# The sample tokens' sparse attention, four tokens at a time in the four column quarters of TensorE's array

## The chip, the cores and the metric

The kernel runs on one core of a Trainium2 chip, as one program. The metric is its time on the device in microseconds (us); less is better. The engines are TensorE (PE in the profile; PEld is its weight load), VectorE (DVE), ScalarE (ACT), GpSimdE (POOL) and SyncE (SP), whose queue issues most of the DMA transfers.

## The reference

One inference step of a four-layer decoder for 512 prompt positions and 8 sample tokens (one new position each, with 512 past positions in a cache). Layers 0 and 3 mix tokens by native sparse attention (NSA), layer 1 by a gated MLP, layer 2 by a linear recurrence (HGRN2); each is followed by a SwiGLU feed-forward block. All is float32. In an NSA layer 16 query heads of 64 channels share 4 key/value heads, and three branches (compressed, selected pages, window) are added under gates. With 512 past positions the nine blocks of 64 are fewer than the sixteen that may be selected, so a sample token reads all its pages. What the change touches is this part, for the 8 sample tokens:

```python
def masked_attend(q, k, v, mask):
    s = jnp.einsum('bqgrd,bkgd->bqgrk', q, k).astype(jnp.float32) * ATTN_SCALE
    p = jnp.where(mask, jax.nn.softmax(jnp.where(mask, s, NEG_INF), axis=-1), 0.0)
    return jnp.einsum('bqgrk,bkgd->bqgrd', p.astype(v.dtype), v), p
...
    s = jnp.einsum('bqgrd,bqgnjd->bqgrnj', q, k_sel).astype(jnp.float32) * ATTN_SCALE
    p = jax.nn.softmax(jnp.where(sel_mask, s.reshape(B, Tq, G, R, -1), NEG_INF), axis=-1)
    o_slc = jnp.einsum('bqgrnj,bqgnjd->bqgrd', p.reshape(s.shape).astype(v_sel.dtype), v_sel)
...
    o_win, _ = masked_attend(q, kw, vw, win_mask[None, :, None, None, :])
    return (gates[:, :, 0, ..., None] * o_cmp + gates[:, :, 1, ..., None] * o_slc
            + gates[:, :, 2, ..., None] * o_win)
```

## The kernel before

Activations lie with features on the 128 partitions and the 520 columns (512 prompt, 8 sample) along them. Every projection multiplies blocks of weights of 128 columns by two halves of the columns (256 and 264), in three passes (`mm`, L248 to L250), on float32r parts whose sum is exact. Weights come by SP's queue (`Weights.dma`, L87) and are split by ScalarE (L100) and VectorE or, beside attention's output projection, by GpSimdE (L101).

An NSA layer (`nsa`) has W_in (21 units of 128 columns, `nsa_in`), attention, and W_out (8 units, `nsa_out`). Attention is written as generators whose steps are put between other instructions by hand; the order of the code's steps is the order of the program, on each engine. `compress` builds the compressed keys and values (L821). `attend` is the prompt's attention by groups, blocks of 128 queries and branches: scores on TensorE (L947, L915), masking and minimum on VectorE (L949), exp on ScalarE (L951), scaling on three engines (L960, L963), transposes (L982), a split by ScalarE and VectorE (L985, L986), and products with the values (L998). Part of it runs beside W_in. After W_in a loop gives one step of `attend` and one of `fill`, which takes steps of `sample` and `compress` in turn, until half the prompt is done; then W_out's first half of columns starts, with four of these steps at each tick (every six projection matmuls).

`sample` is the attention of the 8 sample tokens, on rows (token, head): row 16 b + h, so two tokens lie in each quarter of 32 rows. `begin(1)` and `begin(2)` make the scores and the softmax of the selected pages and of the window, `end(1)` and `end(2)` the products with the values; all add up in one PSUM bank `O`. Scores: for each token `b` and each half `v` of the key channels, one float32 matmul (L1078) of the token's 32 query columns (`Qp`, zero for the other token of the quarter) with its 512 keys, into the 32 PSUM rows of its quarter. Values: for each token and each 128 of its positions, one float32 matmul (`acc`, L1042) of 32 probability columns (`PT`) with 256 value channels. Each matmul uses 32 of the array's 128 columns, the quarter `r = b // 2 * 32`:

```python
for b, t in rows(br, 0):
    kb = t.rearrange("p n (v c) -> p n v c", v=2)
    r = b // 2 * 32
    for v in range(2):
        nc.tensor.matmul(S[r:r + 32], Qp[:, v, b], kb[:, :, v], start=b % 2 == 0 and v == 0,
                         stop=b % 2 == 1 and v == 1)
        yield
```

`rows` loads keys or values on SP's queue, five tokens ahead in the order: four pages of 128 KB for the selected branch (`page`, L763, `cache_slc`), one transfer of 512 KB for the window (L1067, `cache_win`). Tiles named `g` come from one pool of 38 buffers, so a load goes out when the earlier reader of its buffer is done. PSUM tiles (`ps`) come from eight banks.

Of the kernel before, what the change touches and what calls it, by code (L numbers as in the profile page):

```python
# [19 lines left out]
EPS = 1e-5  # L20
CH = (8, 7, 7)
NFF = sum(CH)
SLOTS = 38        # tiles of the pool that nearly everything lives in
WM, WV = 3, 0     # layer norm: ticks before the mean's and the variance's matrix products
# HGRN: order of a head's four projections (q, forget gate, v, output gate), units that run by halves first, ticks
# before a head's levels, levels built ahead, ticks of the sample's part, rate of the last head, output units beside it
HORD, HF, HW, BUILD, SW0, SWAIT, HRATE, EARLY = (0, 1, 2, 3), 6, 1, 3, 0, 8, 2, 6
# NSA: units between scores and mix, blocks between transposes and values, steps that exp and the like are put off
LAG, PVLAG, DEFER = 2, 3, 1
# NSA: steps a tick of attention (beside W_in, beside W_out) and of compression, and of the others for one of attention  # L30
RATE, RATE2, CRATE, STEPS = 4, 4, 1, 1
# NSA: steps that the sample's pages, values and compressed rows are waited for, tokens whose pages load ahead
CWAIT, EWAIT, AHEAD = 8, 5, 5
# [8 lines left out]
def alternate(*gs):  # L42
    """Steps of some generators in turn, until all end."""
    live = list(gs)
    while live:
        for x in list(live):
            try:
                next(x)
                yield
            except StopIteration:  # L50
                live.remove(x)


def wait(n):
    for _ in range(n):
        yield
# [12 lines left out]
class Weights:  # L69
    """Streams weight blocks: DMA, then a split in two float32r parts, ahead of their use."""  # L70
# [46 lines left out]
class Split:  # L117
    """Activations by blocks of features, as two float32r parts whose sum is exact."""
# [25 lines left out]
class Net:  # L144
# [67 lines left out]
    def spawn(self, g, rate=1.0):  # L212
        """A generator whose steps are issued between those of the matrix products."""
        self.par.append([g, rate, 0.0])
        return g
# [21 lines left out]
    def mm(self, unit, nk, R, half, ks=None, p=None):  # L237
        """One 128-column block of weights times the columns of a half: three passes a block of rows."""
        nc = self.nc
# [16 lines left out]
    def order(n, first, last):  # L256
        """(index, half): the first and the last few by halves, the others both halves together."""
# [5 lines left out]
    def ln(self, cols, li, sums, pair, X=None, out=None, direct=False):  # L263
        """Layer norm over the features, in place; its split goes to X, or out(j, c0, c1, pair) follows each pair.
        With direct, the tensor engine alone sums the squares."""
# [61 lines left out]
    def table(self, i):  # L327
        """The set of ScalarE's tables that the next functions need: one set for exp and ln together."""
# [6 lines left out]
    def guess(self, ys, vs):  # L335
        """y = exp(-ln(var + EPS) / 2), guesses at 1 / sqrt(var + EPS)."""
# [6 lines left out]
    def newton(self, ys, vs):  # L343
        """A Newton step from the guesses, and -2 times the results."""
# [19 lines left out]
    def out_proj(self, units, nk, R, scale, li, first=0, last=7, final=False, early=0):  # L364
        """x = scale * x + W h by blocks of features; with li the layer norm runs behind it."""
# [154 lines left out]
    def bounds(self):  # L520
        """The heads' lower bounds of the forget gates, and the norm's gain."""
# [24 lines left out]
    def hgrn(self, layer, plan):  # L546
# [26 lines left out]
        def sample(h, QK, FV, G, S0):  # L573
            """The sample tokens of a head: their states one step on, and what they read from them."""
# [28 lines left out]
        def head(h, QK, FV, G, smp):  # L603
# [6 lines left out]
            def build(i):  # L610
                """Queries times decays from a block's start, keys times decays to its end, by doubling blocks."""
# [23 lines left out]
            def odd(ap, i):  # L635
                """Columns in the second halves of the blocks of a level: its queries."""
# [128 lines left out]
    def nsa(self, layer, plan):  # L765
# [49 lines left out]
        def summaries(cm, n, b):  # L815
            """Compressed keys and values of n pages; with b == 8, of the prompt, whose last page is the position term."""
# [16 lines left out]
        def compress():  # L833
            """Of the prompt first, then of each token's pages."""
# [560 lines left out]
```

## Time and profile before

| | |
|---|---|
| time, median of 3 runs | 3125.0 us (3124.13 to 3129.43) |
| profiled execution: span from first to last instruction | 3127.9 us |
| profiled execution: own time | not given apart from its span |
| TensorE busy | 2960.0 us, 95% |
| VectorE busy | 1734.5 us, 55% |
| ScalarE busy | 1296.0 us, 41% |
| GpSimdE busy | 472.8 us, 15% |
| mean granted clock of TensorE | 0.979 of full speed |
| DMA | 280.61 MB, mean 90 GB/s |

A line of the timeline has the start, the time to the last end, the engine, the line of the code, the operation, what it writes and reads, the shape (weights' rows*columns, then rows x moving columns) and how many records it merges; in brackets stands the idle time ahead of it and what ended it. A float32 matmul gives two records. Ends of matmuls are modelled, so a busy TensorE need not be at its peak.

### The profile page before, as it was taken

What the parts mean: (1) busy time and instruction counts of PE and PEld (TensorE: products, weight loads), DVE (VectorE), ACT (ScalarE), POOL (GpSimd) and SP (SyncE); (2) the same over time, 40 slices, a digit from 0 to 9 for tenths busy, and PEclk for the clock granted to TensorE, in tenths of its full rate; (3) what the DMA queues carried; (4) which work ended last, traced back from release to release, by engine and by line L of the source; (5) the groups of instructions that cost most, each with busy time, mean ns of one, the idle gap of its engine ahead of it and who ended that gap; (6) DMA issues with size and microseconds to landing.
All of it is one profiled execution on the core that took longest, in us unless ns stands there. A gap on an engine that the chain in (4) does not pass through costs nothing. (4 is left out here: it accounts for less than half of the span.)

```text
span 3127.9 us, 56300 instructions
## 1 busy us (share of the span) xinstructions
PE 2960.0 (95%) x22730; PEld 2772.8 (89%) x22730; DVE 1734.5 (55%) x3821; ACT 1296.0 (41%) x2902; POOL 472.8 (15%) x446
## 2 busy tenths in 40 slices
PE   8898999999989999999899999999899999999997
PEld 8887468999988999998899889999888865799997
DVE  4887545333456633337777773333668866543334
ACT  4666434322345431234455443223456655332322
POOL 0222032000030300004222130000312212300002
PEclk9999999999999999999999999999999999999999
DMA  4222433223222222322222222232122143323221
GB/s 170 74 61 84 135 108 102 88 84 107 82 82 95 67 90 92 98 86 78 76 83 76 71 95 88 92 104 82 68 79 66 60 150 91 132 83 100 89 83 40
DMA packets 136039, 280.61 MB, mean 90 GB/s; under 512 B 13026, under 2 KB 76002, under 8 KB 135778
## 3 DMA queue, kind: packets, MB, share of 16 engines
q1 hardware_dynamic: 127168, 261.86, 26.6%
q10 hardware_dynamic: 7458, 10.95, 1.0%
q0 software_dynamic: 1152, 4.19, 0.5%
q8 instruction: 179, 2.93, 0.4%
q14 instruction: 82, 0.67, 0.1%
HBM read 263.69 MB, written 13.27 MB: 89 GB/s over the span
## 5 line engine op out<-in xcount | busy, mean ns | idle before, releaser
L248 PE MATMUL ps<-g 128*128 128x256 f32 (+1 forms) x6176 | 1784.2, 289 | 14.5 <-ACT g L100 13.2
L249 PE MATMUL ps<-g 128*128 128x256 f32 (+1 forms) x6176 | 1755.4, 284 | 6.8 <-DVE g L101 6.8
L250 PE MATMUL ps<-g 128*128 128x256 f32 (+1 forms) x6176 | 1757.1, 285 | 4.4 <-DVE g L271 2.7
L248 PEld LDWEIGHTS ps<-g 128*128 128x128 f32 x6176 | 1177.7, 191 | 37.9 <-ACT g L100 15.0
L249 PEld LDWEIGHTS ps<-g 128*128 128x128 f32 x6176 | 1177.3, 191 | 13.1 <-DVE g L101 8.3
L250 PEld LDWEIGHTS ps<-g 128*128 128x128 f32 x6176 | 1175.1, 190 | 6.1 <-DVE g L271 3.5
L101 DVE TENSOR_TENSOR g<-g 128x512 fp32r<-128x512 f32 (+1 forms) x708 | 468.6, 713 | 59.8 <-ACT g L100 52.5
L100 ACT CAST g<-g 128x512 fp32r<-128x512 f32 (+1 forms) x788 | 426.6, 608 | 118.9 <-DVE g L101 98.0
L419 DVE TENSOR_TENSOR row<-row,ps 128x256 f32<-128x256 f32 (+1 forms) x176 | 74.8, 425 | 515.7 <-PE ps L250 515.7
L209 ACT CAST g<-row 128x256 fp32r<-128x256 f32 (+1 forms) x192 | 78.6, 410 | 503.2 <-DVE row L419 491.6
L360 POOL TENSOR_TENSOR row<-x 128x256 f32<-128x256 f32 (+1 forms) x16 | 13.0, 812 | 1451.7 <-DVE x L383 1331.5
L418 ACT ACTIVATE row<-ps 128x256 f32<-128x256 f32 (+1 forms) x176 | 67.6, 384 | 334.3 <-PE ps L250 334.0
L951 ACT ACTIVATE g<-g,nst 128x128 f32<-128x128 f32 (+3 forms) x256 | 143.1, 559 | 109.8 <-DVE nst L949 109.3
L381 DVE SCALAR_TENSOR_TENSOR x<-x,ps 128x256 f32<-128x256 f32 (+1 forms) x128 | 52.9, 423 | 167.9 <-PE ps L250 167.8
L963 POOL TENSOR_SCALAR g<-g,nst 128x128 f32<-128x128 f32 (+3 forms) x64 | 76.5, 1195 | 442.7 <-DVE nst L956 378.7
L998 PE MATMUL ps<-g 128*128 128x512 f32 x384 | 141.4, 451 | 0.0
L949 DVE CUSTOM_DVE_ANT_0 g<-ps,ncst 128x128 f32<-128x128 f32 (+3 forms) x256 | 119.1, 482 | 39.4 <-PE ps L947 34.1
L947 PE MATMUL ps<-g 128*128 128x256 f32 (+2 forms) x512 | 123.9, 343 | 11.3 <-DVE nst L949 5.9
L985 ACT CAST g<-ps 128x512 fp32r<-128x512 f32 x160 | 91.9, 583 | 102.2 <-PE ps L982 83.2
L101 POOL TENSOR_TENSOR g<-g 128x512 fp32r<-128x512 f32 x80 | 105.0, 1333 | 172.8 <-ACT g L100 170.1
L383 DVE TENSOR_TENSOR x<-x,ps 128x256 f32<-128x256 f32 (+1 forms) x128 | 53.8, 424 | 135.5 <-PE ps L250 135.4
L210 DVE TENSOR_TENSOR g<-row,g 128x256 fp32r<-128x256 f32 (+1 forms) x192 | 81.7, 429 | 83.8 <-ACT g L209 83.8
(239 smaller groups left out, 2954.2 us busy)
## 6 DMA issues: line engine op xcount, KB each, us to landing
g<-ffn_in SPq DMA_DIRECT2D x176, 512.0 KB, 3.6
g<-ffn_out SPq DMA_DIRECT2D x64, 448.0 KB, 3.3
g<-nsa_in SPq DMA_DIRECT2D x42, 512.0 KB, 3.8
cm<-cache_cmp SPq DMA_DIRECT2D x64, 256.0 KB, 3.8
g<-cache_slc SPq DMA_DIRECT2D x128, 128.0 KB, 2.6
g<-cache_win SPq DMA_DIRECT2D x32, 512.0 KB, 6.5
g<-ffn_out SPq DMA_DIRECT2D x32, 512.0 KB, 3.5
g<-hgrn_in SPq DMA_DIRECT2D x32, 512.0 KB, 3.9
```

Of the source, the lines that this page charges most:

```text
L100: self.nc.scalar.copy(h[:, a:b], r[:, a:b])
L101: (self.sub[a > 0] or self.nc.vector).tensor_sub(l[:, a:b], r[:, a:b], h[:, a:b].bitcast(FT))
L209: self.nc.scalar.copy(h, src)
L210: self.nc.vector.tensor_sub(l, src, h.bitcast(FT))
L248: nc.tensor.matmul(p[:, :n], H[:, s], a, start=k == 0, stop=False)
L249: nc.tensor.matmul(p[:, :n], L[:, s], a, start=False, stop=False)
L250: nc.tensor.matmul(p[:, :n], H[:, s], b, start=False, stop=k == nk - 1)
L947: nc.tensor.matmul(p[:, :nn], q, kt[:, s, :nn], start=s == 0, stop=s == 1)
L949: nc.vector.tensor_tensor_reduce(P, p[:, :n], tri[:, 512 - n:], 1.0, 3e38, OP.add, OP.min, st[:, i:i + 1])
L951: defer(lambda P=P, i=i: (self.table(LN_EXP), nc.scalar.activation(P, P, AF.Exp, bias=st[:, i:i + 1], scale=-1.0, accum_out=st[:, 4 + i:5 ...
L985: nc.scalar.copy(PT[:, 0, :512], p)
L998: nc.tensor.matmul(o, v, PT[:, s, :512], start=start and s == 0, stop=stop and s == 1)
```

## The change

`rows` goes through the tokens in the order 0, 2, 4, 6, 1, 3, 5, 7 and gives them out four at a time, the first four when six tokens' loads are issued, the others after the first four's use. `begin` issues, for each four and each `v`, four matmuls next to each other, one in each column quarter; `end` does so for each four and each 128 positions. Ahead of each such group the generator passes two steps in which it issues nothing (`QWAIT`). The changed file also drops comments, and its lines are moved: L1078 is L1083 there, L1042 is L1043, L763 is L764, L1067 is L1068, L982 is L983, L998 is L999, L248 to L250 are L249 to L251.

```diff
-CWAIT, EWAIT, AHEAD = 8, 5, 5
+CWAIT, EWAIT, AHEAD, QWAIT = 8, 5, 5, 2
...
             def rows(br, v):
...
                 ts = []
-                for b in range(8 + AHEAD):
-                    if b < 8:
-                        t = self.flat()[:, :1024].rearrange("p (n c) -> p n c", n=4)
-                        if br == 1:
-                            for n in range(4):
-                                self.page(4 * b + n, t[:, n, :], a["cache_slc"][lj, v])
-                        else:
-                            nc.sync.dma_start(t, a["cache_win"][lj, v, b])
-                        ts.append(t)
-                    if b >= AHEAD:
-                        yield b - AHEAD, ts.pop(0)
+                for i, b in enumerate((0, 2, 4, 6, 1, 3, 5, 7)):
+                    t = self.flat()[:, :1024].rearrange("p (n c) -> p n c", n=4)
+                    if br == 1:
+                        for n in range(4):
+                            self.page(4 * b + n, t[:, n, :], a["cache_slc"][lj, v])
+                    else:
+                        nc.sync.dma_start(t, a["cache_win"][lj, v, b])
+                    ts.append((b, t))
+                    if i == AHEAD:
+                        yield ts[:4]
+                        del ts[:4]
+                yield ts
 
             def begin(br):
                 S = self.ps()
-                for b, t in rows(br, 0):
-                    kb = t.rearrange("p n (v c) -> p n v c", v=2)
-                    r = b // 2 * 32
+                for four in rows(br, 0):
                     for v in range(2):
-                        nc.tensor.matmul(S[r:r + 32], Qp[:, v, b], kb[:, :, v], start=b % 2 == 0 and v == 0,
-                                         stop=b % 2 == 1 and v == 1)
+                        yield from wait(QWAIT)
+                        for b, t in four:
+                            kb = t.rearrange("p n (v c) -> p n v c", v=2)
+                            r = b // 2 * 32
+                            nc.tensor.matmul(S[r:r + 32], Qp[:, v, b], kb[:, :, v], start=b % 2 == 0 and v == 0,
+                                             stop=b % 2 == 1 and v == 1)
                         yield
...
-                for b, vb in values:
-                    r = b // 2 * 32
+                for four in values:
                     for n in range(4):
-                        acc(O[r:r + 32, :256], PT[:, n, b], vb[:, n])
+                        yield from wait(QWAIT)
+                        for b, vb in four:
+                            r = b // 2 * 32
+                            acc(O[r:r + 32, :256], PT[:, n, b], vb[:, n])
                         yield
```

**TensorE, first scores of the selected pages in layer 0.** The scores are written to `ps_3829`; `g_3830` holds the keys of token 0, `g_3835` those of token 1 before and of token 2 in the change; L982 and L998 (L983 and L999) are attention's transposes and products. Before:

```order
L1078 MATMUL ps_3829<-g_3830,g_3824 32x512
L982 MATMUL ps_3861<-ident_85,g_3579 128x128 x2
L982 MATMUL ps_3861<-ident_85,g_3580 128x128 x2
L998 MATMUL ps_3576<-g_3629,g_3000 128x512 x2
L1078 MATMUL ps_3829<-g_3830,g_3824 32x512
L982 MATMUL ps_3880<-ident_85,g_3579 128x128 x2
L982 MATMUL ps_3880<-ident_85,g_3580 128x128 x2
L998 MATMUL ps_3576<-g_3644,g_3000 128x512 x2
L1078 MATMUL ps_3829<-g_3835,g_3824 32x512 x2
```

In the change:

```order
L1083 MATMUL ps_3829<-g_3830,g_3824 32x512
L1083 MATMUL ps_3829<-g_3835,g_3824 32x512
L1083 MATMUL ps_3829<-g_3840,g_3824 32x512
L1083 MATMUL ps_3829<-g_3845,g_3824 32x512
L983 MATMUL ps_3923<-ident_85,g_3579 128x128 x2
L983 MATMUL ps_3923<-ident_85,g_3580 128x128 x2
L999 MATMUL ps_3930<-g_127,g_125 128x512 x2
L983 MATMUL ps_3943<-ident_85,g_3579 128x128 x2
L983 MATMUL ps_3943<-ident_85,g_3580 128x128 x2
L999 MATMUL ps_3930<-g_3865,g_3000 128x512 x2
```

Four matmuls on four tokens stand next to each other where one stood, and attention's instructions follow in a block.

**TensorE, values of the window in layer 0,** in W_out's first half; `g_4988`, `g_4990`, `g_4992` are tokens 0, 1, 2 before; `g_4871` to `g_5012` are tokens 1, 3, 5, 7 in the change. Before:

```order
L1042 MATMUL ps_3828<-g_4988,g_4948 32x256 x2
L1042 MATMUL ps_3828<-g_4990,g_4948 32x256 x2
L248 MATMUL ps_4967<-g_4554,g_4863 128x256
L249 MATMUL ps_4967<-g_4554,g_4864 128x256
L250 MATMUL ps_4967<-g_4555,g_4863 128x256
L248 MATMUL ps_4967<-g_4554,g_4863 128x256
L249 MATMUL ps_4967<-g_4554,g_4864 128x256
L250 MATMUL ps_4967<-g_4555,g_4863 128x256
L1042 MATMUL ps_3828<-g_4990,g_4948 32x256 x2
L1042 MATMUL ps_3828<-g_4992,g_4948 32x256 x2
```

In the change:

```order
L1043 MATMUL ps_3828<-g_4869,g_4780 32x256
L249 MATMUL ps_4995<-g_4557,g_4907 128x256
L250 MATMUL ps_4995<-g_4557,g_4908 128x256
L251 MATMUL ps_4995<-g_4558,g_4907 128x256
L249 MATMUL ps_4995<-g_4557,g_4907 128x256
L250 MATMUL ps_4995<-g_4557,g_4908 128x256
L251 MATMUL ps_4995<-g_4558,g_4907 128x256
L1043 MATMUL ps_3828<-g_4871,g_4780 32x256
L1043 MATMUL ps_3828<-g_4873,g_4780 32x256
L1043 MATMUL ps_3828<-g_5010,g_4780 32x256
L1043 MATMUL ps_3828<-g_5012,g_4780 32x256
L1043 MATMUL ps_3828<-g_4871,g_4780 32x256
```

Before, the two value matmuls of one token stand next to two of the token after it, in the same quarter or the next one; in the change each group has one of each quarter.

**SP, loads around the values of the window in layer 0.** Before:

```order
L87 DMA g_4869<-nsa_out 128x1024
L87 DMA g_4965<-nsa_out 128x1024
L1067 DMA g_4988<-cache_win 128x1024
L1067 DMA g_4990<-cache_win 128x1024
L1067 DMA g_4992<-cache_win 128x1024
L1067 DMA g_4994<-cache_win 128x1024
L1067 DMA g_4996<-cache_win 128x1024
L1067 DMA g_4998<-cache_win 128x1024
L1067 DMA g_5010<-cache_win 128x1024
L1067 DMA g_5022<-cache_win 128x1024
L87 DMA g_5034<-ffn_in 128x1024
```

In the change:

```order
L1068 DMA g_4863<-cache_win 128x1024
L1068 DMA g_4865<-cache_win 128x1024
L1068 DMA g_4867<-cache_win 128x1024
L1068 DMA g_4869<-cache_win 128x1024
L1068 DMA g_4871<-cache_win 128x1024
L1068 DMA g_4873<-cache_win 128x1024
L88 DMA g_4913<-nsa_out 128x1024
L88 DMA g_4993<-nsa_out 128x1024
L1068 DMA g_5010<-cache_win 128x1024
L1068 DMA g_5012<-cache_win 128x1024
L88 DMA g_5061<-ffn_in 128x1024
```

The window's last two loads (tokens 5 and 7) have moved behind two blocks of W_out.

## Rows read from the trace of the kernel before

**Rows 1.** The page, its table of engines: busy us, share of the span, instructions.

```profile
PE 2960.0 (95%) x22730; PEld 2772.8 (89%) x22730; DVE 1734.5 (55%) x3821; ACT 1296.0 (41%) x2902; POOL 472.8 (15%) x446
```

**Rows 2.** TensorE groups by line, 2530 to 2700 us (second NSA layer), two costliest.

```profile
L1042 PE MATMUL ps<-g 128*32 128x256 f32 (+2 forms) x136 | 33.3, 388 | 1.4 <-ACT g L1117 1.4
L1078 PE MATMUL ps<-g 128*32 128x512 f32 x64 | 30.9, 601 | 1.0 <-DVE g L1037 1.0
```

**Rows 3.** Timeline of TensorE, first NSA layer: start, us, line, out<-in, records.

```profile
345.50 1.90 PE L1078 MATMUL ps<-g 128*32 128x512 f32 x4
347.33 0.51 PE L947 MATMUL ps<-g 128*128 128x256 f32 x2
347.76 1.05 PE L1078 MATMUL ps<-g 128*32 128x512 f32 x2
348.74 0.61 PE L972 MATMUL ps<-ident,g 128*32 128x128 f32 x4
...
353.99 1.90 PE L1078 MATMUL ps<-g 128*32 128x512 f32 x6
355.82 1.14 PE L915 MATMUL ps<-g 128*128 128x192 f32 x8
...
365.36 0.62 PE L947 MATMUL ps<-g 128*128 128x384 f32 x2
...
374.61 1.73 PE L1042 MATMUL ps<-g 8*128 8x256 f32 x3 [1.39 <-ACT g L1117]
```

**Rows 4.** Timeline, 353.98 to 354.05 us alone: weight loads (PEld) and matmuls begun there.

```profile
353.99 0.15 PEld L1078 LDWEIGHTS ps<-g 128*32 128x32 f32 x4
353.99 0.63 PE L1078 MATMUL ps<-g 128*32 128x512 f32 x2
```

**Rows 5.** Timeline of TensorE, values of the window, first NSA layer.

```profile
439.23 1.91 PE L1042 MATMUL ps<-g 128*32 128x256 f32 x8
441.08 0.39 PE L248 MATMUL ps<-g 128*128 128x256 f32 x1
...
441.98 1.06 PE L1042 MATMUL ps<-g 128*32 128x256 f32 x8
442.98 0.39 PE L248 MATMUL ps<-g 128*128 128x256 f32 x1
```

**Rows 6.** Timeline of TensorE, a lone value matmul, first NSA layer.

```profile
389.47 0.62 PE L1042 MATMUL ps<-g 128*32 128x256 f32 x2
390.02 0.66 PE L982 MATMUL ps<-ident,g 128*128 128x128 f32 x4
```

**Rows 7.** Stretches: span, busy us of PE, PEld, DVE, ACT, POOL; clock, DMA, GB/s.

```profile
308.90:345.50 36.60, 36.55 (x177) 19.44 (x177) 17.95 (x65) 14.01 (x40) 1.31 (x2) 1.00 0.60 192
345.50:356.90 11.40, 11.40 (x42) 4.05 (x41) 8.61 (x34) 7.48 (x22) 2.12 (x3) 1.00 0.01 4
356.90:374.60 17.70, 15.75 (x72) 8.65 (x71) 10.52 (x34) 7.66 (x20) 1.48 (x2) 1.00 0.58 170
374.60:388.20 13.60, 13.03 (x42) 6.45 (x42) 8.03 (x24) 6.68 (x17) 1.99 (x2) 0.62 0.30 89
388.20:430.00 41.80, 41.22 (x220) 24.92 (x220) 26.37 (x51) 20.18 (x42) 15.52 (x13) 1.00 0.17 51
2604.20:2613.00 8.80, 8.23 (x42) 4.37 (x42) 7.70 (x24) 6.52 (x17) 1.98 (x2) 1.00 0.48 138
```

**Rows 8.** A stretch without sample matmuls, columns as in rows 7.

```profile
366.18:374.61 8.43, 6.47 (x42) 5.17 (x41) 6.36 (x23) 5.70 (x16) 0.74 (x1) 1.00 0.82 237
```

**Rows 9.** Timeline of SP, loads of pages and windows, first NSA layer.

```profile
329.09 11.50 SPq L1067 DMA_DIRECT2D g<-cache_win  x8
360.86 17.55 SPq L763 DMA_DIRECT2D g<-cache_slc  x32
```

**Rows 10.** The page, DMA issues: count, KB each, median us to landing.

```profile
g<-cache_slc SPq DMA_DIRECT2D x128, 128.0 KB, 2.6
g<-cache_win SPq DMA_DIRECT2D x32, 512.0 KB, 6.5
g<-ffn_out SPq DMA_DIRECT2D x32, 512.0 KB, 3.5
```

## The prediction

> **What bounds the kernel now.** First the page's table of engines: TensorE is busy for 95% of the span, VectorE for 55%, ScalarE 41%, GpSimdE 15% [rows 1]. So time taken off TensorE shortens the run, unless another engine or a transfer is late in that place. Then the groups by line in the second NSA layer: the sample tokens' scores (L1078) hold TensorE for 30.9 us there, their values (L1042) for 33.3 us, and TensorE's idle time ahead of all the groups shown is some 4 us [rows 2]. Both layers together spend about 128 of 3127.9 us on these two lines, with an array of which 32 of 128 columns are used.
>
> Third, the timeline, for what neighbours cost. I count from a start to the next line's start, since a matmul's modelled end overlaps the next start by 0.07 us. A float32 matmul is two records (two passes over the moving columns). One score matmul: 347.76 to 348.74, 0.98 us; two on the same token, so in one column quarter: 345.50 to 347.33, 1.83 us. Hence 0.43 us a pass and 0.12 us for entering and leaving the 32-column form. At 353.99 six records stand together, two matmuls of token 3 (quarter 1) and one of token 4 (quarter 2): they take 353.99 to 355.82, again 1.83 us [rows 3]. The third matmul cost nothing. For values: eight records in one quarter take 1.85 us (439.23 to 441.08), eight in two quarters 1.00 us (441.98 to 442.98) [rows 5]; a lone value matmul takes 0.55 us (389.47 to 390.02) [rows 6]. So two quarters already run side by side in this kernel, wherever the order happens to put them next to each other. The change makes that the rule, and with four.
>
> Fourth, the stretches of the first layer, for what stands behind TensorE: from 308.9 to 374.6 us VectorE is busy 17.95 + 8.61 + 10.52 = 37.1 of 65.7 us, from 388.2 to 430 us 26.4 of 41.8 us [rows 7]. It has room now; with a third of TensorE's work gone it has little.
>
> **The sum, a layer; there are two.** *Scores.* 64 records in 23 places: 30.9 - 23 x 0.07 = 29.3 us of path. After: 8 fours (two branches, two fours, two halves of the key channels). The four tokens' passes run beside each other, so a four is one matmul's 0.98 us plus three later starts. Two matmuls of different quarters begin within the first 0.06 us of that place, with four weight loads [rows 4]; I allow 0.02 us for all: 1.00 us, 8.0 us in all. Removed: 21.3.
>
> *Values.* 136 records in 34 places: 33.3 - 34 x 0.07 = 30.9 us, of which eight full-width records (1.9 us) stay: 29.0. After: 16 fours of 0.55 + 0.04 = 0.59, so 9.4 us. Removed: 19.6. Together **40.9 us a layer, 81.8 in both**. What four quarters cost isn't in the trace; two do. The bounds are a four at the price of one matmul (above) and at the price of two after each other, 1.83 and 1.00 us, which takes back 8 x 0.83 + 16 x 0.41 = 13.2 us a layer. I take the first, since two quarters show no slowing at all (1.00 us for four passes of 0.216).
>
> *The waits put in* (two idle steps ahead of each four) issue nothing. A branch's scores go from 16 steps to 12 and its values from 32 to 24, and in the order the sample's last instruction stays in the same output-projection unit, so no step is left over for the end. The transposes, softmax and page bytes stay as they are: nothing.
>
> *What comes back, by stretch.*
> (a) 308.9 to 374.6: TensorE's other work is 65.7 - 29.3 - 2.0 (waits) = 34.4 us; with eight fours 42.4, against VectorE's 37.1 [rows 7]. How attention goes without sample matmuls between is seen from 366.18 to 374.61: 8.43 us for 6.47 us of TensorE, a factor of 1.30; VectorE is busy for 6.36 of it [rows 8]. Bounds: fours that fill every gap, 42.4; none, 34.4 x 1.30 + 8.0 = 52.7. The fours are spread over the first two thirds, so I take 46: **3.6 us** back (0 to 10.3).
> (b) The selected pages' values: 32 page loads leave SP in 17.55 us, 0.55 each, and one lands 2.6 us after its issue [rows 9, 10]. The first four reads 16 pages: 16 x 0.55 + 2.6 = 11.4 us after the first issue. Token by token only four were needed, 4.8 us. By the waits of the built program the tiles now come free with the last score four; from the last score to the first values it was 9.2 us (365.36 to 374.61 [rows 3]), and the order has about the same work there. 11.4 - 9.2: **2 us** back (0 to 6).
> (c) 374.6 to 388.2 is slowed in the first layer: granted clock 0.62, so partly at 1.2 GHz and not 2.4. The same work takes 8.8 us in the second layer, where VectorE is busy for 7.70 of it [rows 7]. TensorE's 8.23 less nine value matmuls of 0.55 and plus five fours of 0.59 is 6.2, VectorE's 7.7 stays: **1 us** back.
> (d) 388.2 to 430: TensorE's 41.2 less 23 value matmuls of 0.55 and plus three fours is 30.3, VectorE's 26.4 [rows 7]: close, but the projection's matmuls fill gaps. **1 us** back (0 to 4).
> (e) The window's values. In SP's new order the last two window loads stand behind two blocks of W_out, and their tiles are freed by the last attention products, some 2.2 us of TensorE's work ahead of the four that reads them. A window load lands 6.5 us after its issue (the median, in bursts), a weight load of the same 512 KB 3.5 [rows 10]. So 1.3 to 4.3 us; for the first four, whose third load's tile is freed about 3 us ahead, 0.5 to 3.5. I take 2.5 + 1.5 = **4 us**. Queued behind that wait on TensorE are W_out's matmuls, and behind the loads on SP the first blocks of the next layer's W_in, which are not due for units.
> Sum: 11.6 us a layer, 23.2 in both.
> (f) The clock: in the first layer it fell after TensorE had been busy for 6.47 of 8.43 us [rows 8], and cost 4.8 us (13.6 against 8.8 [rows 7]). The changed kernel waits more. From that row: a gain of 4.8 if this fall goes, a loss of 9.6 with two more. I take 3 us lost.
> 81.8 - 23.2 - 3 = 55.6. The profiled span of 3127.9 us lies 2.9 above the median of 3125.0 and inside the three runs (3124.13 to 3129.43); no other time of that execution is given, so the difference is taken off the median: **3069 us**.
>
> **A rule of the skill that speaks against it.** [Rows 3 and 4] show token 4's first pass starting 0.01 us after token 3's first, ahead of three passes of token 3 that stand earlier in the program; its weights are loaded by then. The Trainium skill ("TensorE: Matmul & The Clock Gate", Part 3, The mechanism) says that matmuls start and end strictly in program order, and that weights load beside a running matmul only where the row groups differ; here all tokens use all 128 rows. By it a four would be no faster than the second rival below makes it; the trace disagrees for two quarters, and no run here yet shows four.
>
> **Rivals.**
> 1. *Attention becomes the bound.* Where the sample no longer fills, TensorE waits for VectorE, ScalarE and its eight banks at the fill-free factor of 1.30: (a) loses 10.3 (and covers (b)), (c) 1, (d) 4, (e) its upper end of 7.8: a layer keeps 17.8, and with 3 for the clock 3125 - 35.6 + 3 is about 3092. For it: [rows 8]. Against: the fours and the compression matmuls still stand between. Chance 0.15.
> 2. *In program order.* If no pass may overtake, a token's second pass starts only after its first, and the next token's first can run beside that second: five passes for a four. 5 x 0.43 + 0.12 = 2.27 for scores, 5 x 0.216 + 0.12 = 1.20 for values, 37.4 us a layer where 17.4 stand above. 20 us a layer less, while TensorE, being longer, hides most of (a) to (e): 81.8 - 40 - 8 = 34, about 3091. Against: [rows 3, 4]. Chance 0.05.
> 3. *Two quarters at a time*, 13.2 us a layer less with some 4 us a layer less in waits: 81.8 - 26.4 - 15 - 3 = 37, about 3088. Chance 0.06.
> 4. *Every four waits for its loads* (slower than before). A four needs four tokens landed, and if their tiles only come free when the last four is done, nothing is loaded ahead: 11.4 us for 16 pages, and for four window tokens half of 11.5 us [rows 9] and 6.5 to land, 12.3 us. Eight page fours and eight window fours: 190 us in all, less what other work covers. It outweighs the 81.8 when the mean wait of the 16 passes 5.1 us; with half exposed: 3125 - 82 + 95 = 3138. Against: six of eight tokens are ordered ahead, as before. Chance 0.03.
> 5. *Nothing comes back*: 3125 - 82, about 3043; with a little, 3050. Chance 0.08.
> The forecast, 3053 to 3085, has 0.63.
>
> **How the numbers follow.** The range of 3047 to 3097 holds the forecast, rivals 2 and 3, most of 1 and half of 5; what it leaves out is 4, the rest of 5 and the tail of 1. A measurement of this kernel tells about 0.2% (6 us) from no change; all cases but 4 are faster by more than that. Faster 0.95, same 0.02, slower 0.03.
>
> **What would show it.** Scores in 8 and values in 16 places a layer, with 8 records each, at about 1.00 and 0.59 us from start to next start: that tells the forecast from rivals 2 and 3. TensorE's waits between the first four and the end of the sample: about 10 us a layer more, on VectorE and ScalarE in the attention stretch, on loads of cache_slc ahead of the first values and of cache_win ahead of the fifth window four. Waits for loads over 5 us in each four would mean rival 4, VectorE over 90% busy in (a) rival 1. The forecast is wrong if a four takes over 1.5 us, or if the waits in both layers pass 50 us.

## The result, and the profile after

The changed kernel takes 3077.9 us (median of 4 runs, 3075.7 to 3078.4) where the kernel before takes 3127.0: a ratio of 0.9844, 95% interval 0.9831 to 0.9857. It is faster by 1.6%, some 49 us of the 55.6 that were forecast, and inside the range of 3047 to 3097. (The kernel before was run again 21 times beside the experiments, with medians of 3123.4 to 3124.7; from those the gain is 46 us.) The profiled executions have spans of 3127.9 and 3076.7 us, 51.2 apart. The page's table of engines, to be held against [rows 1]:

```profile
PE 2886.1 (94%) x22730; PEld 2759.4 (90%) x22730; DVE 1725.9 (56%) x3821; ACT 1293.8 (42%) x2902; POOL 473.4 (15%) x446
```

TensorE is busy for 73.9 us less, but the span fell by 51.2 only: 22.7 us more are idle (190.6 for 167.9). The busy time has the clock in it too, since a matmul in a stretch at the lower level takes about twice as long (two score records from 325.03 on, shown below, take 1.82 us at a granted clock of 0.50, and one such matmul 0.98 at 1.00 [rows 3]). The granted clock was 0.5 for 128.4 us of the span before and for 148.7 after. I call busy time less half of that the *work*: 2895.8 before, 2811.7 after. So by this account the 51.2 us are **84.1 of work removed, 10.2 given back to the clock, 22.7 given back to waits**.

The account separates the three only roughly. TensorE idles in part of the low stretches; with half of their busy part alone (54.3 and 63.4 us) it reads 83.0, 9.1 and 22.7. And waits and clock stand in for each other: over the 48 executions of the twelve changed kernels below, one that has 1 us more of half low clock than its kernel's mean (by its mean granted clock) is only 0.3 us longer, with a standard error of 0.1. Half of the low-clock time is therefore an upper price.

**The fours.** The timeline of TensorE in the first NSA layer after the change (columns as in [rows 3]):

```profile
315.18 1.06 PE L1083 MATMUL ps<-g 128*32 128x512 f32 x8
...
358.02 0.64 PE L1043 MATMUL ps<-g 128*32 128x256 f32 x8
358.59 0.62 PE L948 MATMUL ps<-g 128*128 128x384 f32 x2
```

Eight records, which is four tokens' matmuls, take 1.00 us (the next start is 0.997 later, at 316.17) for scores and 0.57 us for values. One token's matmul took 0.98 and 0.55 [rows 3, 6]. A window of 0.07 us from the start of that value four:

```profile
358.02 0.16 PEld L1043 LDWEIGHTS ps<-g 128*32 128x32 f32 x8 [0.25 <-issue]
358.02 0.42 PE L1043 MATMUL ps<-g 128*32 128x256 f32 x4
```

All eight weight loads and the first pass of all four tokens begin within it; before, two quarters did so by chance [rows 4].

**The waits.** What TensorE waited for from 300 to 450 us, before (us in total, times, longest):

```profile
PE ps L1042 <- ACT g L1117: 1.4, 1, 1.4
PE ps L1078 <- DVE g L1037: 1.1, 1, 1.1
PE ps L250 <- DVE g L210: 0.6, 1, 0.6
PE ps L947 <- DVE nst L949: 0.6, 1, 0.6
PE ps L248 <- ACT g L209: 0.6, 1, 0.6
```

and after:

```profile
PE ps L1043 <- DMA g<-cache_win: 4.3, 4, 1.8
PE ps L1083 <- DMA g<-cache_slc: 3.5, 2, 1.9
PE ps L249 <- ACT g L210: 3.3, 1, 3.3
PE ps L1157 <- DVE g L1153: 3.0, 1, 3.0
PE ps L250 <- POOL g L102: 2.5, 1, 2.5
PE ps L948 <- DVE g L1121: 1.0, 1, 1.0
...
```

In order of time these are: the third four of the selected pages' scores (cache_slc); the start of W_out (L249, on ScalarE's copy of attention's output in `split`, L210); the transposes of the compressed branch (L1157, on VectorE's softmax); the window's value fours (cache_win); and a weight block that GpSimdE splits (L102) beside the output projection, after the sample's end. In the second layer the same lines wait 1.6, 3.3, 3.0, 4.0 and 2.5 us.

Why the third four waits is seen in TensorE's timeline and in SP's:

```profile
319.49 1.05 PE L1083 MATMUL ps<-g 128*32 128x512 f32 x4
322.10 1.02 PE L1083 MATMUL ps<-g 128*32 128x512 f32 x2 [1.56 <-DMA g<-cache_slc]
325.03 1.89 PE L1083 MATMUL ps<-g 128*32 128x512 f32 x2 [1.91 <-DMA g<-cache_slc]
```

```profile
297.75 13.62 SPq L764 DMA_DIRECT2D g<-cache_slc  x24
312.22 4.90 SPq L764 DMA_DIRECT2D cm<-cache_cmp  x4
317.47 4.07 SPq L764 DMA_DIRECT2D g<-cache_slc  x8
```

`rows` orders six tokens (24 pages) ahead. The last two are ordered only when the first two fours are issued, behind four loads of the compressed cache, so the last page leaves SP at about 321.5. The four falls apart: the two tokens that have landed go at 319.49, the third at 322.10 and the last at 325.03, and TensorE does nothing else meanwhile. Token by token, the same two would have been due last.

**The clock.** Stretches of the first layer after (columns as in [rows 7]):

```profile
317.00:323.60 6.60, 4.56 (x26) 2.42 (x24) 2.14 (x7) 2.46 (x8) 0.00 (x0) 1.00 0.78 228
323.60:330.40 6.80, 5.37 (x18) 2.78 (x22) 1.87 (x11) 1.82 (x7) 0.71 (x1) 0.50 0.45 156
371.40:374.80 3.40, 3.40 (x18) 2.27 (x18) 2.36 (x7) 1.12 (x3) 0.75 (x1) 0.50 0.02 5
391.90:395.30 3.40, 3.40 (x15) 2.90 (x14) 1.84 (x6) 1.50 (x4) 0.00 (x0) 0.50 0.00 0
422.60:426.00 3.40, 3.40 (x17) 1.75 (x16) 0.00 (x0) 0.00 (x0) 0.00 (x0) 0.50 0.05 19
```

Each of the four stretches at 0.50 (1.2 GHz of 2.4) begins in one of the waits above or within 2 us of its end: at the third four, at the start of W_out (TensorE idle 3.33 us up to 369.97 and 0.71 more up to 371.18), behind the transposes of the compressed branch (idle 3.02 up to 391.48), behind the window's fifth four. The kernel before had one long fall here, at 374.7, and [rows 8] showed the idle time ahead of it; that one is gone. Both NSA stretches (290 to 500 and 2430 to 2720 us) hold 30.8 us of low clock before and 54.6 after. All executions bear it out: the mean granted clock is 0.976 over the changed kernel's four, and 0.979 to 0.980 over each set of seven of the kernel before.

### The profile page after: what moved, and what is told of

Same layout as the page of the kernel before. It is cut to its first block, busy times and chain, and to the rows that moved or that the text cites. A ratio compares the mean times of both kernels' runs of the same rounds, so it can differ in the third digit from the quotient of the medians.

```text
span 3076.7 us, 56298 instructions
## 1 busy us (share of the span) xinstructions
PE 2886.1 (94%) x22730; PEld 2759.4 (90%) x22730; DVE 1725.9 (56%) x3821; ACT 1293.8 (42%) x2902; POOL 473.4 (15%) x446
## 5 line engine op out<-in xcount | busy, mean ns | idle before, releaser
L249 PE MATMUL ps<-g 128*128 128x256 f32 (+1 forms) x6176 | 1784.8, 289 | 19.5 <-ACT g L101 12.9
L250 PE MATMUL ps<-g 128*128 128x256 f32 (+1 forms) x6176 | 1758.0, 285 | 10.9 <-DVE g L102 5.8
L251 PE MATMUL ps<-g 128*128 128x256 f32 (+1 forms) x6176 | 1759.1, 285 | 3.0 <-DVE g L211 1.7
L249 PEld LDWEIGHTS ps<-g 128*128 128x128 f32 x6176 | 1180.2, 191 | 34.6 <-ACT g L101 13.3
L250 PEld LDWEIGHTS ps<-g 128*128 128x128 f32 x6176 | 1179.7, 191 | 18.3 <-DVE g L102 7.1
L251 PEld LDWEIGHTS ps<-g 128*128 128x128 f32 x6176 | 1177.5, 191 | 4.6 <-DVE g L211 2.6
L102 DVE TENSOR_TENSOR g<-g 128x512 fp32r<-128x512 f32 (+1 forms) x708 | 467.6, 711 | 59.9 <-ACT g L101 52.5
L210 ACT CAST g<-row 128x256 fp32r<-128x256 f32 (+1 forms) x192 | 78.6, 410 | 503.4 <-DVE row L420 491.7
L999 PE MATMUL ps<-g 128*128 128x512 f32 x384 | 142.1, 452 | 1.2 <-DVE g L987 0.9
L102 POOL TENSOR_TENSOR g<-g 128x512 fp32r<-128x512 f32 x80 | 105.7, 1342 | 162.4 <-ACT g L101 147.6
L316 POOL TENSOR_SCALAR x<-x,lngn,lngb 128x256 f32<-128x256 f32 (+1 forms) x120 | 104.8, 886 | 144.7 <-ACT g L312 129.9
```

What stands on the lines that cost most here:

```text
L102: (self.sub[a > 0] or self.nc.vector).tensor_sub(l[:, a:b], r[:, a:b], h[:, a:b].bitcast(FT))
L210: self.nc.scalar.copy(h, src)
L249: nc.tensor.matmul(p[:, :n], H[:, s], a, start=k == 0, stop=False)
L250: nc.tensor.matmul(p[:, :n], L[:, s], a, start=False, stop=False)
L251: nc.tensor.matmul(p[:, :n], H[:, s], b, start=False, stop=k == nk - 1)
L316: nc.gpsimd.tensor_scalar(xs[:, k], xs[:, k], g, b, op0=OP.mult, op1=OP.add)
```

## The experiments

Their account, each from its profile: work, idle time and half of the low-clock time add up to the span. The experiments' ratios are to the kernel before run beside them (3123 to 3125 us). One profile stands for each kernel, and the clock differs where the programs are alike, too: between the two NSA layers (530 to 2400 us) it is low for 51 us in the profile of experiment 6 and for 77 in that of 9. So a few us in the last column mean little.

| kernel | median us | ratio (95%) | work | idle | half of low clock |
|---|---|---|---|---|---|
| before | 3127.0 | | 2895.8 | 167.9 | 64.2 |
| the change | 3077.9 | 0.9844 (0.9831 to 0.9857) | 2811.7 | 190.6 | 74.4 |
| 1 two quarters | 3079.9 | 0.9859 (0.9842 to 0.9875) | 2831.4 | 176.0 | 71.2 |
| 2 scores only | 3084.1 | 0.9868 (0.9851 to 0.9884) | 2857.2 | 168.4 | 59.1 |
| 3 values only | 3108.3 | 0.9947 (0.9931 to 0.9964) | 2856.9 | 183.6 | 68.0 |
| 4 all loads ahead | 3061.4 | 0.9804 (0.9787 to 0.9820) | 2811.5 | 182.2 | 66.4 |
| 5 loads ahead, two quarters | 3080.3 | 0.9857 (0.9840 to 0.9873) | 2835.8 | 178.3 | 64.5 |
| 6 loads ahead, tail | 3065.4 | 0.9813 (0.9797 to 0.9830) | 2808.2 | 182.8 | 67.7 |
| 7 no empty steps | 3077.7 | 0.9852 (0.9835 to 0.9868) | 2805.4 | 191.2 | 79.8 |
| 8 loads, tail, two more | 3048.5 | 0.9754 (0.9736 to 0.9773) | 2810.8 | 176.4 | 58.9 |
| 9 as 8, steps alone | 3056.5 | 0.9777 (0.9761 to 0.9794) | 2805.2 | 170.6 | 79.6 |
| 10 as 8, distance alone | 3058.5 | 0.9787 (0.9770 to 0.9803) | 2805.8 | 177.8 | 71.3 |
| 11 as 8, without tail | 3064.4 | 0.9803 (0.9786 to 0.9819) | 2806.5 | 184.4 | 73.3 |

**1. Two quarters at a time.** Tokens in their old order, so that a four lies in two quarters:

```diff
-                for i, b in enumerate((0, 2, 4, 6, 1, 3, 5, 7)):
+                for i, b in enumerate(range(8)):
```

> The changed kernel with the tokens in the order 0 to 7, so that a group of four lies in two column quarters, two tokens in each. Theory (quarters run side by side, a quarter takes its passes one after the other): a score group takes 1.83 us and a value group about 1.0 in place of 1.00 and 0.57; 13.5 us a layer more on TensorE, of which some 4 are hidden in waits: about 3096 us (3088 to 3105). Rival (the gain is from standing together, fewer entries into the 32-column form, and not from four quarters): within 5 us of the changed kernel's 3078.

TensorE's timeline, a four of scores and one of values; then the first 0.07 us of that score four alone:

```profile
313.86 1.92 PE L1083 MATMUL ps<-g 128*32 128x512 f32 x8
...
354.43 1.06 PE L1043 MATMUL ps<-g 128*32 128x256 f32 x8
```

```profile
313.86 0.63 PE L1083 MATMUL ps<-g 128*32 128x512 f32 x2
```

The fours take 1.85 and 0.99 us to the next start, as two quarters were to; the work is 19.7 us more than with four. But the time is the change's within 2 us, which is the rival's number and not the 3096 expected. The fours' lengths speak against the rival's reason, since all of them stand together here as well. The idle time fell by 14.6: a longer four covers waits that the shorter one leaves open. Those for loads are 6.6 us shorter in the two layers, that at the start of W_out, which is on ScalarE, 4.2. Experiment 5 tests the part of the loads.

**2 and 3. Scores alone, values alone.** The other part keeps the kernel before's `rows`, under the name `rows1`, and its loop. Of scores alone:

```diff
-                values = rows(br, 1)
+                values = rows1(br, 1)
...
-                for four in values:
+                for b, vb in values:
```

> Only the scores in fours; the values token by token, as before. Theory (21.3 us of scores a layer are removed, some 5 a layer come back as waits for pages and VectorE): about 33 us under the kernel before, 3094 (3088 to 3100), and scores and values add up to about the 49 us of the whole change. Rival (VectorE bounds attention once both are removed): scores alone keep nearly all of their 42.6 us, 3086 or less, and the two parts together come to over 60 us.

> Only the values in fours; the scores token by token, as before. Theory (19.6 us a layer are removed, about 12 a layer come back: the window's loads 4, the first block of W_out 3, the compressed branch's softmax 3, GpSimd's split 2.5): about 16 us under the kernel before, 3111 (3104 to 3117). Rival (VectorE bounds attention only when both are removed): 30 us or more under it, 3097 or less.

Scores alone gain 39.7 us (medians), values alone 15.5, for the same 39 us of work each. The values came as expected; the scores missed the range, at the rival's number. The difference lies in waits and clock: values alone wait 15.7 us longer than the kernel before and scores alone 0.5, and half of the low clock moves by +3.8 and -5.1. The sum, 55, is more than the whole change's 46 beside the same kernel before, but not over the 60 of the rival. By the account the whole adds 6.5 us more of waits than the two parts together, and 11.5 more of clock; it also removes 6.6 us more of work than they do, and nothing here says why. So the terms are not good to better than that.

**4. All eight tokens ordered before the first four.**

```diff
-                    if i == AHEAD:
+                    if i == 7:
```

> The changed kernel with all eight tokens' loads ordered before the first four's use (six before). Theory (the waits for loads in the second four of the first scores, 1.6 to 3.5 us, and of the window's values, 2.0 to 2.7 us, come from the last two loads' place in SP's order): both waits go, 8 us less in both layers: 3070 (3065 to 3074). Rival (buffers and the issue time of SP set when loads land, not their place in the order): waits only move to the first four, within 4 us of the changed kernel.

It gains 16.4 us on the change, twice what was expected: by the account 8.4 of waits and 8.0 of clock, 6.8 of that in the two NSA stretches. The third four has no idle time left ahead of its tokens, though its last one still starts late, at 320.50, so that it takes 1.97 us and not 1.00; the stretch after it runs at full clock. The window's first four still waits, 1.4 and 2.0 us; its fifth waits no more. TensorE's timeline, SP's, and the stretch that had the clock of 0.50 in the change:

```profile
319.48 2.05 PE L1083 MATMUL ps<-g 128*32 128x512 f32 x8
321.45 0.97 PE L948 MATMUL ps<-g 128*128 128x256 f32 x6
```

```profile
297.75 20.90 SPq L764 DMA_DIRECT2D g<-cache_slc  x32
318.89 2.76 SPq L764 DMA_DIRECT2D cm<-cache_cmp  x4
```

```profile
323.60:330.40 6.80, 6.73 (x59) 5.80 (x51) 4.42 (x21) 4.64 (x15) 1.37 (x2) 1.00 0.95 333
```

So this fall of the clock hung on the waits at the third four: 3.5 us of them, and then 6.8 us at the lower level, cost up to twice their length. The other profiles agree. Where two waits stand there (1.7 and 1.8 us in experiment 2, 2.2 and 2.3 in 7) the clock falls for 6.8 us as well (from 324.5 and 319.2 on); with one of 1.5 us (1) or none (the others) it does not fall there.

**5. The fourth with two quarters** (the edits of 1 and 4).

> All eight tokens' loads ordered ahead, and the tokens in the order 0 to 7 (two quarters a group). Theory (two quarters cost little in e1 because their 13.5 us a layer filled waits, for loads above all, that four quarters leave open): with the loads ahead those waits are gone, so four quarters now win clearly: 3074 us (3068 to 3081) against 3061. Rival (attention's own chain on VectorE and ScalarE bounds the layer, whatever TensorE saves beyond two quarters): within 5 us of 3061.

Here two quarters lose 18.8 us to four, as expected. With experiment 1 this settles it: the gain of four over two is real (24.3 us of work) and was hidden for the most part by late loads: with the loads ahead four quarters gain 16.4 us and two none (3080.3 for 3079.9).

**6. The two waits of the tail.** On top of 4, seven steps in place of two ahead of the compressed branch's transposes, and no split on GpSimdE after the compressed branch's end:

```diff
-                yield from wait(2)
+                yield from wait(7)
...
             yield from comp_end()
+            self.W.sub = (None, None)
```

> All loads ahead, and two of the other waits taken on: the compressed branch's transposes seven idle steps behind its softmax in place of two (wait 3.0 us a layer), and the weights' second split back on VectorE as soon as the sample's last step is issued (wait for GpSimd 2.5 us a layer). Theory (each wait is paid in full and nothing stands behind it): 11 us less than 3061, 3050 (3047 to 3055). Rival (the next instruction on the same engine waits in its place): within 4 us of 3061.

TensorE's waits, 300 to 450 us:

```profile
PE ps L1043 <- DMA g<-cache_win: 3.5, 2, 2.3
PE ps L249 <- ACT g L210: 3.4, 1, 3.4
PE ps L983 <- ACT g L1159: 2.4, 1, 2.4
...
PE ps L250 <- DVE g L102: 0.7, 1, 0.7
```

The wait behind the split falls from 2.5 to 0.7 (now on VectorE), so that edit does what it was to do, and L1157 waits no more. But this came out as the rival says: the prompt's next transposes (L983) wait 2.4 us for ScalarE's copy of the compressed branch's (L1159), and the window's values wait 3.5 where they waited 1.4 in experiment 4. The time is no better (4 us longer, where 11 less were expected).

**7. No empty steps ahead of the fours:** `QWAIT = 0`.

> The changed kernel without the two empty steps ahead of each four (QWAIT 0), six tokens loaded ahead as in the change. Theory (the empty steps give the loads time to land; without them each second four stands nearer to its loads): 2 to 4 us more of wait at each of the four places a layer, 3090 us (3083 to 3100). Rival (loads are set by buffers and SP's issue times, and the steps only move work): within 4 us of 3078.

The same time as the change (3077.7), as the rival says and not the theory. The waits move from the values to the scores (cache_slc 5.6 us for 3.5 in the first layer, cache_win not among the largest). The two empty steps neither gain nor lose.

**8. More distance at the two waits that were left.** On top of 6, six steps of `fill` (the sample's, and those of `compress` while it lasts) after W_out's first operand is put, and four more empty steps ahead of the window's values. In the code these four stand ahead of the window's loads, too, since `rows` orders the first load when `end` first asks it for a four. In time the distance grows all the same, since TensorE gets to the values later: from the first of these loads on SP to the first of the values it is 6.0 us in experiment 6, 8.4 in 10 and 7.3 in 8.

```diff
         run(put(0))
+        step(fill, 6)
...
-                yield from wait(EWAIT)
+                yield from wait(EWAIT if br == 1 else EWAIT + 4)
```

> As e6, and six steps of the sample issued behind the first split of W_out's input (TensorE waits 2.4 to 3.3 us there), and four more idle steps ahead of the window's first values (waits of 1.4 to 2.0 us for loads). Theory: TensorE has two value fours to do in the first wait (1.1 us) and the loads land in the second: 5 us less than e6, 3045 (3040 to 3050). Rival (the two moved fours wait for their own pages, or the time is taken from later cover): within 3 us of e6.

It is the fastest of all, 3048.5 us: 75 under the kernel before beside it, 29 under the change. TensorE's waits, 300 to 450 us:

```profile
PE ps L249 <- ACT g L210: 2.5, 1, 2.5
...
PE ps L1043 <- DMA g<-cache_win: 0.6, 1, 0.6
```

The gain over 6 was 17 us where about 5 were expected. Between the two profiles, of which that of 6 is of its fastest execution, it is 12.6: 6.4 less idle, 8.8 less half-clock time, 2.6 more work. Not all of that clock is the edits': the clock is low for 17.5 us less, and before 290 us, where the programs are alike, for 17.0 less; in the two NSA stretches it is 10.2, in the rest 9.7 more.

**9 to 11. The parts of 8** ("the last run" of the expectations is experiment 8; the edits are shown above).

> The sixth run's kernel with one of the two edits of the last run alone: six of sample's steps after the first unit of W_out. Theory that this edit covers the wait at the start of W_out (3.4 us a layer in the sixth run) and nothing else: that wait falls to 1.0 to 2.5 us, the values of the window still wait 3.5 and 2.3 us for their loads and the compressed branch's transposes 2.4 us, the time falls by 2 to 5 us from the sixth run's 3065 to 3061 (3059 to 3064). Rival, that it alone made most of the 17 us of the last run: 3052 or less, with the window's waits under 1.5 us a layer.

> The sixth run's kernel with the other of the two edits alone: four more empty steps between the window's loads and its values. Theory: the window's values no longer wait for loads (3.5 and 2.3 us in the sixth run's two layers, under 1.0 each then), the wait at the start of W_out stays at 3.4 us a layer, and the time falls by the 4 to 5 us of these waits and up to 5 us of low clock that follows them, to 3058 (3054 to 3062). Rival, that it alone made most of the last run's gain: 3052 or less. Second rival, that the steps only shift the values to a place where they wait for something else: 3065 within 3 us.

> The last run's kernel without the two edits that the sixth run added to the fourth (seven steps in place of two ahead of the compressed branch's transposes; no GpSimd splits after its end). If those two edits gain nothing, as the sixth run's 3065 beside the fourth's 3061 says, the time is the last run's 3048 or a little less (3043 to 3051). Rival: the two waits they were meant for come back (3.0 us for VectorE and 2.5 us for GpSimd a layer), 11 us in the two layers, 3059 (3055 to 3063).

(The expectation of 10 has the four steps between the loads and the values; they stand ahead of both, as said at 8.) Steps alone gain 8.9 us on 6, distance alone 6.9, and together 17.0, so they add; steps alone gained more than expected (also at the window's values, which wait 2.7 there), distance alone what was expected. Without the edits of 6, however, the same two gain nothing on experiment 4 (2.9 us longer, with executions that overlap). That expectation missed: TensorE waits 3.1 us for the window's loads again and 2.3 for GpSimdE's split, 8.0 us more idle than in 8. Edits that gained nothing by themselves became worth 16 us when the next waits behind them were gone. Why 9 isn't the fastest stays open. Its profile has less idle time than that of 8 and much more low clock (159 us for 118), but it is of the one execution with a mean clock of 0.974; the two at 0.979 are no faster (3055.8 and 3059.1 us, where those of 8 at 0.979 take 3042.0 and 3050.4).

## Why the prediction came out

The sign and the range were right, and the likeliest time, 3069, was 9 us too low. By its steps:

- **The price of a four: right.** 1.00 us forecast and measured for scores, 0.59 forecast and 0.57 measured for values, wherever the four tokens had landed and the clock was at its upper level, in 8 places and (two fours standing together once) 15 places a layer. The work removed is 84.1 us where 81.8 were forecast. Reading the neighbours by chance [rows 3 to 5] was enough to know it.
- **Rivals 2 and 3: refuted by the same rows.** Four first passes begin within 0.07 us. In program order a four would have taken 2.27 and 1.20 us; two quarters at a time it takes 1.85 and 0.99 (experiment 1). The rule that starts and ends of matmuls keep the program's order (the Trainium skill, "TensorE: Matmul & The Clock Gate", Part 3, The mechanism) doesn't hold for column quarters here. Experiment 1 shows it most plainly: of the score four at 313.86 two records begin at once, and since the passes of one quarter go one after the other, 0.43 us apart, they are token 0's and token 2's; token 1's matmul, which stands between them in the program, cannot begin before 0.88 us. In a four of the change the matmuls begin in their order, and only the first passes overtake second passes.
- **(a) and (b), 5.6 us a layer: nothing of it came as forecast.** From the first score to the first value it takes 41.23 us in the second layer, load waits and all, and 39.48 in the first with all loads ahead (experiment 4), TensorE busy for 38.55 of it and VectorE for 30.23. In the change's own first layer it takes 46.21. That is near the 46 taken for (a), but it comes from the third four's waits and the low clock with them. The wait ahead of the first selected values (1.4 us before) is gone, too: 32 pages are ordered early enough. Rival 1 is refuted, with VectorE at 77% and not over 90.
- **What the sum left out: the stretch itself got shorter.** It is below the lower bound of 42.4 because less stands in it. The two rows below are from the first score to the first value, before and after (columns as in [rows 7]):

```profile
308.95:374.61 65.66, 63.70 (x288) 32.14 (x288) 37.04 (x130) 29.16 (x80) 4.93 (x6) 1.00 0.49 154
309.64:355.85 46.21, 40.86 (x261) 26.17 (x260) 30.28 (x111) 23.40 (x67) 4.24 (x5) 0.93 0.61 191
```

  The sample's two scores have 12 steps each in place of 16, and attention's steps are threaded between them. So some 27 of attention's records on TensorE and 6.8 us of VectorE's work now come behind the first value. The prediction names the 12 steps, but keeps 34.4 us of TensorE's other work in (a) and VectorE's work in (c) and (d) as it was.
- **(c) and (d), 2 us a layer: some 8 came.** The start of W_out waits 3.3 (0.6 before), the compressed branch 3.0, GpSimdE's split 2.5. The prediction priced these stretches by VectorE's busy time over the whole of them. In the first two waits VectorE is indeed the full engine, for 3.74 of 4.00 and 2.85 of 3.00 us:

```profile
366.00:370.00 4.00, 0.67 (x10) 0.18 (x9) 3.74 (x11) 3.15 (x8) 1.37 (x1) 1.00 0.02 7
388.50:391.50 3.00, 0.02 (x1) 0.03 (x1) 2.85 (x10) 1.34 (x3) 2.38 (x2) 1.00 0.48 175
```

  So the cause was right in kind and its size wrong: a mean over the stretch hides the places where TensorE has nothing else in front of it. In the third wait (435.5 to 438 us) GpSimdE is at its split, busy for 1.96 of 2.50 us. Experiments 6 and 8 show that these waits shrink when TensorE is given other steps first or another engine does the split (the start of W_out still waits 2.5 us in the first layer of 8). That the moved work made VectorE late is the reading that fits, not shown by itself.
- **(e), 4 us a layer: right** (4.3 and 4.0), in the places named: 1.6 and 2.0 at the first four, where 1.5 were taken, and 2.7 and 2.0 at the fifth, where 2.5 were.
- **Missed: the scores' third four** (3.5 and 1.6 us). The prediction found this very mechanism for the window's values, two loads ordered late for a four that needs them, and rested its case against rival 4 on "six of eight tokens are ordered ahead", without carrying it to the pages. (Rival 4 did not come: of the 24 fours of a layer these three wait for loads. Nor did rival 5.)
- The waits are 22.7 us together, 23.2 forecast. That agreement is luck: 15.4 and 13.0 us in the two layers (the gaps over 0.1 us), not 11.6 each, and 5.7 us fewer elsewhere, which I haven't traced.
- **(f), the clock, is the term of the sum that was mis-sized:** by the account 10.2 us lost where 3 were taken; in the two NSA stretches alone it is 11.9. It was priced by the one fall of the kernel before, as a cost of its own. Experiment 4 shows for one place that the fall comes with the waits: without the one, the other is gone, too. Over the whole change it is 10.2 us for 22.7 of waits, 0.45 for each. At that price the prediction's own 23.2 us of waits cost 10.4, and 81.8 - 23.2 - 10.4 = 48.2 gives 3077; that is the run's own price put back in, and no test of it.

What stays open: why the clock falls after one such wait and not after another of the same length (the compressed branch's 3.0 us bring a fall in both layers of the change, and in experiment 4 in the second alone). Executions of one kernel differ in it (mean clock 0.973 to 0.978 in experiment 10, 3054 to 3061 us), so a few us between two of these kernels mean little.

## What to carry to other kernels

Work that uses a quarter of the array's columns can be put beside other such work by order alone, and the trace of a kernel that does it once by chance gives the price. When pieces are grouped, a group is due when its last operand has landed: order all loads of a group before the first use of the group ahead, or the faster group waits. When the pieces are given out in fewer steps, whatever was threaded between the steps moves as well: count again what stands in each stretch. After taking work away, read each hand-written distance between a result and its use again, in microseconds and not in steps, all of them together, since removing one wait only uncovers the next.

## What the runs showed of the hardware

- Four float32 matmuls of 32 columns in four column quarters cost as much as one: 1.00 us against 0.98 (512 moving columns), 0.57 against 0.55 (256). Eight weight loads begin within 0.07 us. In two quarters a matmul begins 0.87 us ahead of one that stands before it in the program (experiment 1).
- A wait of TensorE can cost more than itself: in the first layer of the change the clock falls in or behind four waits, to 1.2 GHz for 3.4 to 6.8 us each. In experiment 4 the waits at one of these places are gone, and so is its fall of 6.8 us. Not each wait of the same length has one.
- A longer operation on the bottleneck can cost next to nothing where it covers waits: two quarters instead of four were 19.7 us more work and 2 us more time, and 18.8 us more time once the loads were early (experiments 1 and 5).
